# Attention output and forward keys of a gated linear attention block, turned by VectorE and trips through HBM in place of TensorE

## The chip, the cores and the metric

The kernel runs on one core of a Trainium2 chip. The time is the device time of one execution in microseconds; three runs of the kernel before are given. The profile is of one further execution, taken by the hardware profiler. Engines are PE (TensorE), DVE (VectorE), ACT (ScalarE), POOL (GpSimd) and SP (SyncE), which issues the DMAs.

## The reference, cut to what matters

One block over 1024 tokens of width 1024, all in float32. The input projection gives q, k (4 heads of 128), v, r (4 heads of 256), low-rank decays, a pooling input and two merge gates. The part around the change is the attention branch:

```python
def gla_chunked(q, k, v, log_a, include_diag):      # per head, in chunks
    b = jnp.cumsum(log_a...)                        # inside a chunk
    q_e = q * jnp.exp(b)
    k_e = k * jnp.exp(-b)
    k_d = k * jnp.exp(b_last - b)
    scores = jnp.where(mask, q_e @ k_e^T, 0.0)
    kv = k_d^T @ v                                  # sum over the chunk's tokens
    # state_{n+1} = exp(b_last) * state_n + kv_n
    return scores @ v + q_e @ state

o = gla(q, k, v, a_fwd, True) + flip(gla(flip(q), flip(k), flip(v), flip(a_bwd), False))
o = o * lax.rsqrt(jnp.mean(o * o, axis=-1, keepdims=True) + EPS)   # per head
o = o * gla_norm * silu(r)
y_a = o @ w_branch_gla
```

Two axes matter. The sum in kv runs over tokens, so keys are needed with tokens on the partitions, while q, k and their decays are computed with features on the partitions. The attention output o comes out with tokens on the partitions (the norm runs along its row), while `silu(r)` and the product with `w_branch_gla` want it with features there.

## The kernel before, in words

Tokens come in 8 tiles of 128 (two halves of 4), features in tiles of 128. Every float32 operand of a large product is split into a high and a low part; a product is three matmuls of 512 columns (hh x wh, hl x wh, hh x wl; `products` and `mm3`, line L273). Line L200 is the ACT cast that makes a high part, L201 the subtraction that makes the low part, on DVE or POOL (`split_to` for kt and p; the weights' wh and wl alike).

The order on each engine is written by hand. The main code runs the projections (q and k, v, then r, then the gates). After each three matmuls it calls `pump`, which advances the queues of side work: `side` (generators such as `attention(h)`; a `yield x` lets x units of main work pass before the next step), `aside`, `pending` and `put_off`. All engines execute in that order; SP too issues its DMAs in it, and each waits there for what it needs. `later` puts a store on a list, `flush` issues the list. Working tiles of 4 KB a row come from a pool of 39 (`slot`).

`attention(h)` runs for heads 0 to 3 in turn beside the projections; their backward loops begin at about 96, 160, 225 and 286 us. Its steps: the decays (la, z; with the scan of L851), the decayed q and k (qe, ke; d=0 is forward, d=1 backward), `transposed_keys` (four PE transposes into the PSUM tile kp, split into kt), then the backward loop n = 7 to 1. `advance` there takes kv on PE, st on DVE (L911, L913), and on ACT the state for this chunk sb (L917) and for the next step so (L921). Then `scores` (sc, its masking and its split p), and the forward loop n = 0 to 7: op on PE (p with v, then sb, then sf), another `advance`, the copy o (L999) on DVE, its squares (L1000) on ACT. `rms_scale` (DVE and a power on POOL) gives ors. The scalings by it (`normalize`, L1019) run in the next head, after its Exp, with stores to `o_out` by `flush`; in the last head they run at once, and o stays in SBUF.

The r projection (about 287 to 383 us) runs by feature tile j and half. For j below 3 the result is copied (`r`, L1236) and put by; from j = 3 each step does one of those and its own in `gated`: Silu on ACT, four PE transposes of o into the PSUM tile tp (L1188), one DVE instruction (L1195) that multiplies tp, the norm's weight and Silu(r). `load_o` reads heads 0 to 2 back as ol ahead of j = 2, 3, 4. Beside this stage run the gate projection's weights and sums (fraw, fs, L1093), and results of gates go through ga (L1474). Results of `gated` are stored to `ob_out`.

## Time and profile before

| | us |
|---|---|
| runs, median (lowest to highest) | 1374.98 (1374.72 to 1375.22) |
| span of the profiled execution | 1373.4 |
| PE busy | 1361.4 (99%) |
| DVE busy | 836.8 (61%) |
| POOL busy | 752.1 (55%) |
| ACT busy | 647.3 (47%) |

The profiled execution's own time is its span, 1373.4; the runs' median stands 1.6 above it. A row of the timeline reads: start, duration, engine, line, operation, output <- inputs, shape, count, and in brackets the idle time before it with the instruction that ended it. A row of a group reads: line, engine, operation, count | total, mean ns of one | idle time before, releaser. A row on a tile gives ns minimum/median/maximum and the first and last start. A window's row gives busy times of PE, PE's weight loads, DVE, ACT and POOL, then the granted clock, the DMA share and GB/s. Durations on one engine overlap a little, since an instruction starts before the one ahead has quite ended.

### The profile page before, as it was taken

What the parts mean: (1) busy time and instruction counts of PE and PEld (TensorE: products, weight loads), DVE (VectorE), ACT (ScalarE), POOL (GpSimd) and SP (SyncE); (2) the same over time, 40 slices, a digit from 0 to 9 for tenths busy, and PEclk for the clock granted to TensorE, in tenths of its full rate; (3) what the DMA queues carried; (4) which work ended last, traced back from release to release, by engine and by line L of the source; (5) the groups of instructions that cost most, each with busy time, mean ns of one, the idle gap of its engine ahead of it and who ended that gap; (6) DMA issues with size and microseconds to landing.
All of it is one profiled execution on the core that took longest, in us unless ns stands there. A gap on an engine that the chain in (4) does not pass through costs nothing. (4 is left out here: it accounts for less than half of the span.)

```text
span 1373.4 us, 17879 instructions
## 1 busy us (share of the span) xinstructions
PE 1361.4 (99%) x6310; PEld 1132.9 (82%) x6310; DVE 836.8 (61%) x1034; ACT 647.3 (47%) x1177; POOL 752.1 (55%) x557
## 2 busy tenths in 40 slices
PE   9999999999999999999999999999999999999998
PEld 7888888888888888888888888888888888888886
DVE  6974556554735777678883955655566556343375
ACT  7365666755534445554346533333333334444253
POOL 3323723222597547667764376666676667455454
PEclk9999999999999999999999999999999999999999
DMA  6321523314778569995416355555544447985451
GB/s 227 113 87 52 181 90 92 95 60 123 245 236 278 186 198 308 373 386 216 150 71 241 112 174 176 176 176 177 176 145 137 146 136 266 384 301 187 169 215 77
DMA packets 167834, 251.97 MB, mean 183 GB/s; under 512 B 11160, under 2 KB 94144, under 8 KB 167744
## 3 DMA queue, kind: packets, MB, share of 16 engines
q1 hardware_dynamic: 167600, 250.57, 53.8%
q8 instruction: 49, 0.80, 0.2%
q14 instruction: 41, 0.34, 0.1%
q10 hardware_dynamic: 144, 0.26, 0.0%
HBM read 168.74 MB, written 82.05 MB: 183 GB/s over the span
## 5 line engine op out<-in xcount | busy, mean ns | idle before, releaser
L201 POOL TENSOR_TENSOR wl<-fs,wh 128x512 fp32r<-128x512 f32 x124 | 173.1, 1400 | 163.5 <-ACT wh L200 104.0
L273 PE MATMUL ps<-gh,wh 128*128 128x512 f32 x616 | 240.5, 390 | 0.0
L273 PE MATMUL ps<-gl,wh 128*128 128x512 f32 x616 | 239.8, 389 | 0.3 <-DVE gl L1691 0.3
L273 PE MATMUL ps<-gh,wl 128*128 128x512 f32 x616 | 239.7, 389 | 0.0
L201 POOL TENSOR_TENSOR wl<-fraw,wh 128x512 fp32r<-128x512 f32 x93 | 134.0, 1442 | 75.0 <-ACT wh L200 72.4
L201 POOL TENSOR_TENSOR ol<-gor,oh 128x1024 fp32r<-128x1024 f32 (+1 forms) x42 | 101.3, 2417 | 86.0 <-ACT oh L200 71.7
L273 PE MATMUL ps<-hh,wh 128*128 128x512 f32 x356 | 145.1, 408 | 0.7 <-ACT ga L1474 0.7
L273 PE MATMUL ps<-hh,wl 128*128 128x512 f32 x356 | 139.0, 390 | 0.0
L273 PE MATMUL ps<-hl,wh 128*128 128x512 f32 x356 | 138.8, 390 | 0.0
L273 PEld LDWEIGHTS ps<-gl,wh 128*128 128x128 f32 x616 | 115.7, 188 | 24.5 <-DVE gl L1691 0.7
L273 PEld LDWEIGHTS ps<-gh,wh 128*128 128x128 f32 x616 | 115.7, 188 | 24.1 <-ACT hb L1710 0.2
L273 PEld LDWEIGHTS ps<-gh,wl 128*128 128x128 f32 x616 | 115.7, 188 | 23.9
L273 PE MATMUL ps<-oh,oh 128*128 128x512 f32 x308 | 119.8, 389 | 0.0
L273 PE MATMUL ps<-ol,oh 128*128 128x512 f32 x308 | 119.8, 389 | 0.0
L273 PE MATMUL ps<-oh,ol 128*128 128x512 f32 x308 | 119.8, 389 | 0.0
L201 POOL TENSOR_TENSOR wl<-wraw,wh 128x512 fp32r<-128x512 f32 x56 | 92.3, 1679 | 44.7 <-ACT wh L200 44.6
L201 POOL TENSOR_TENSOR wl<-raw,wh 128x512 fp32r<-128x512 f32 x34 | 47.4, 1404 | 108.3 <-ACT wh L200 71.9
L201 DVE TENSOR_TENSOR ol<-wor,oh 128x1024 fp32r<-128x1024 f32 (+1 forms) x42 | 62.8, 1506 | 68.1 <-ACT oh L200 55.5
L200 ACT CAST wh<-fs 128x512 fp32r<-128x512 f32 x124 | 76.1, 615 | 29.5 <-DVE fs L1093 28.3
L273 PEld LDWEIGHTS ps<-hh,wl 128*128 128x128 f32 x356 | 66.8, 188 | 14.4
L273 PEld LDWEIGHTS ps<-hh,wh 128*128 128x128 f32 x356 | 67.0, 188 | 13.1 <-ACT ga L1474 1.1
L273 PEld LDWEIGHTS ps<-hl,wh 128*128 128x128 f32 x356 | 67.0, 188 | 12.0
(281 smaller groups left out, 3073.4 us busy)
## 6 DMA issues: line engine op xcount, KB each, us to landing
fraw<-in_w_ffn_in_dram SPq DMA_DIRECT2D x44, 512.0 KB, 6.1
gor<-g_out SPq DMA_DIRECT2D x35, 512.0 KB, 6.1
fraw<-in_w_in_dram SPq DMA_DIRECT2D x22, 512.0 KB, 6.5
g_out<-s SPq DMA_DIRECT2D x44, 256.0 KB, 2.3
wor<-t_out SPq DMA_DIRECT2D x20, 512.0 KB, 3.7
raw<-in_w_in_dram SPq DMA_DIRECT2D x36, 256.0 KB, 5.1
g_out<-g SPq DMA_DIRECT2D x33, 256.0 KB, 2.6
x<-in_x_dram SPq DMA_DIRECT2D x16, 512.0 KB, 5.6
```

The costliest lines, as they stand in the source:

```text
L200: nc.scalar.copy(hi, src)
L201: eng.tensor_tensor(lo, src, as_f32(hi), op=ALU.subtract)
L273: nc.tensor.matmul(ps, a[i], b[j], start=first and n == 0, stop=last and n == 2, skip_group_check=onto)
```

## The change

Two kinds of transposes leave PE. A transpose of a 128x512 tile is instead made of two steps: DVE turns each 32x32 block in place (STREAM_TRANSPOSE), and four stores, one for each group of 32 partitions, write the blocks to their places in HBM in runs of 512 bytes; a load brings the tile back with the other axis on the partitions, its columns in blocks of 32.

- Forward keys (d=0): `turn_keys` after the backward keys of half 0 and at n = 6 of the backward loop, `put_keys` (4 stores of 64 KB) at n = 7 and 4, `get_keys` (256 KB) at n = 5 and 1, `split_keys` at n = 1 and in the forward loop at n = 2. The backward keys keep `transposed_keys`.
- Output: `turn` scales two tiles and turns them; half 0 in the forward loop (n = 5, 6), half 1 in the next head where `normalize` stood, in two steps. Each half is stored by 4 DMAs of 128 KB (two stores of 512 KB per head before). The last head's output goes the same way now: its stores are kept in `last_o` and issued at j = 4 of the r projection, and `load_o(3)` follows at j = 5. The rms scale is taken in two halves.
- `gated` has no PE transposes; four DVE instructions of 128x4x32 read the loaded tile and Silu(r), both in SBUF.

```diff
+        def turn_keys(half, d):
+            both = slot(s="kq")
+            nc.vector.transpose(
+                both[:, 0, :].rearrange("p (j c b) -> p c j b", j=4, b=SQ),
+                ke[half][:, d, :].rearrange("p (c j a) -> p c j a", j=4, a=SQ),
+            )
+            turned_k[half, d] = both
+        def put_keys(half, d):
+            to = k_out[h, half, d].rearrange("(j a) (i m) -> i a j m", a=SQ, i=4)
+            for i in range(4):
+                src = turned_k[half, d][i * SQ : (i + 1) * SQ, 0, :]
+                nc.sync.dma_start(to[i], src.rearrange("p (j m) -> p j m", j=4))
+        def get_keys(half, d):
+            nc.sync.dma_start(turned_k[half, d][:, 1, :], k_out[h, half, d])
+        def split_keys(half, d):
+            kt = slot(F32R, s="kt")
...
+            split_to(hi, lo, back)
+            kts[half, d] = kt
...
         kts[0, 1] = transposed_keys(0, 1)
+        turn_keys(0, 0)
...
             if n == 7:
                 apply_decay(1, 0)
+                put_keys(0, 0)
+            elif n == 6:
+                turn_keys(1, 0)
+            elif n == 5:
+                get_keys(0, 0)
+            elif n == 4:
+                put_keys(1, 0)
+            elif n == 1:
+                split_keys(0, 0)
+                get_keys(1, 0)
             yield 1.2
             if n == 3:
-                kts[0, 0] = transposed_keys(0, 0)
                 yield 0.5
...
+        def turn(half, part):
...
+            for i in range(2 * part, 2 * part + 2):
+                t = o[half][:, i, :]
+                nc.vector.tensor_scalar(t, t, scales[half][:, i : i + 1], None, op0=ALU.mult)
+            nc.vector.transpose(
+                turned[half][:, :, :].rearrange("p k (n b) -> p n k b", b=SQ)[:, two],
+                o[half][:, two, :].rearrange("p n (k a) -> p n k a", a=SQ),
+            )
+            if part:
+                to = o_out[h][half].rearrange("(k a) (i m) -> i a k m", a=SQ, i=4)
+                for i in range(4):
+                    (last_o if h == HEADS - 1 else deferred).append((to[i], turned[half][i * SQ : (i + 1) * SQ, :, :]))
...
             if n == 0:
                 yield 0.38
-                kts[1, 0] = transposed_keys(1, 0)
...
+            if n == 2:
+                split_keys(1, 0)
             if n == 3:
                 p = q_next
+                scales[0] = rms_scale(ms[:, :4], 4, "ors")
+            if n in (5, 6):
+                turn(0, n - 5)
...
-        tp = bank(ps_g, "tp")
-        for i in range(4):
-            nc.tensor.transpose(
-                tp[:, i * P : (i + 1) * P],
-                o_heads[j // 2][half][:, i, (j % 2) * P : (j % 2 + 1) * P], ident[:, :],
-            )
...
+        for i in range(4):
+            nc.vector.scalar_tensor_tensor(
+                every(tiles[half][:, j % 2, :], i), turned[:, i], g_gla[:, j : j + 1], every(sr[:, :], i),
+                op0=ALU.mult, op1=ALU.mult,
+            )
...
             if half == 0:
                 flush()
+                if j == 4:
+                    deferred.extend(last_o)
+                    flush()
+                elif j == 5:
+                    load_o(HEADS - 1)
```

What moves on the engines, at the three places that matter most. First SP in head 3, from its weights to the loads of earlier heads' output (raw is a piece of weights, ol an output read back, k_out and kq the turned keys in HBM and in SBUF). Before:

```order
L208 DMA raw_2832<-in_w_in_dram 128x4x128
L208 DMA raw_2834<-in_w_in_dram 128x4x128
L1033 DMA ol_2961<-o_out_565 128x1024
L1033 DMA ol_2962<-o_out_565 128x1024
L208 DMA raw_2965<-in_w_in_dram 128x4x128
L208 DMA raw_2967<-in_w_in_dram 128x4x128
L1033 DMA ol_3151<-o_out_566 128x1024
L1033 DMA ol_3152<-o_out_566 128x1024
L208 DMA raw_3155<-in_w_in_dram 128x4x128
L208 DMA raw_3157<-in_w_in_dram 128x4x128
```

and now:

```order
L209 DMA raw_2898<-in_w_in_dram 128x4x128
L209 DMA raw_2900<-in_w_in_dram 128x4x128
L926 DMA k_out_571<-kq_2999 32x4x128 x4
L1091 DMA ol_3033<-o_out_573 128x2x512
L1091 DMA ol_3034<-o_out_573 128x2x512
L209 DMA raw_3037<-in_w_in_dram 128x4x128
L209 DMA raw_3039<-in_w_in_dram 128x4x128
L929 DMA kq_2999<-k_out_571 128x512
L926 DMA k_out_572<-kq_3055 32x4x128 x4
L929 DMA kq_3055<-k_out_572 128x512
L1091 DMA ol_3218<-o_out_574 128x2x512
L1091 DMA ol_3219<-o_out_574 128x2x512
```

Ahead of the first ol and of the raw behind it now stand the four stores of half 0's turned keys.

Second ACT in head 3, the last four steps of the backward loop (wh and raw: weights of the r projection; kt: split keys; p: split scores). Before:

```order
L200 CAST wh_3010<-raw_2965 128x512
L917 ACTIVATE sb_2946<-st_3018,fac_2859 128x256
L921 ACTIVATE so_3021<-st_3018,fac_2859 128x256
L200 CAST wh_3029<-raw_2967 128x512
L200 CAST kt_3038<-kp_3033 128x512
L917 ACTIVATE sb_2946<-st_3045,fac_2859 128x256
L921 ACTIVATE so_3048<-st_3045,fac_2859 128x256
L917 ACTIVATE sb_2946<-st_3057,fac_2859 128x256
L1236 COPY r_2969<-ps_2970 128x512
L200 CAST p_3078<-sc_3069 128x512
```

and now:

```order
L201 CAST wh_3089<-raw_3037 128x512
L951 ACTIVATE sb_3014<-st_3097,fac_2925 128x256
L955 ACTIVATE so_3100<-st_3097,fac_2925 128x256
L201 CAST wh_3108<-raw_3039 128x512
L951 ACTIVATE sb_3014<-st_3116,fac_2925 128x256
L955 ACTIVATE so_3119<-st_3116,fac_2925 128x256
L951 ACTIVATE sb_3014<-st_3128,fac_2925 128x256
L201 CAST kt_3131<-kq_2999 128x512
L1300 COPY r_3041<-ps_3042 128x512
L201 CAST p_3153<-sc_3144 128x512
```

The cast of kt has left the middle of the loop and stands behind its last sb, and reads the tile loaded from HBM (kq) instead of kp.

Third DVE in head 2, the end of the forward loop (from the st of n = 3 on; o is the copy of the output). Before:

```order
L913 SCALAR_TENSOR_TENSOR st_2598<-kv_2594,fac_2273,so_2580 128x256
L999 COPY o_2493<-op_2588 128x256
L913 SCALAR_TENSOR_TENSOR st_2623<-kv_2619,fac_2318,so_2601 128x256
L999 COPY o_2494<-op_2613 128x256
L913 SCALAR_TENSOR_TENSOR st_2644<-kv_2640,fac_2318,so_2626 128x256
L999 COPY o_2494<-op_2634 128x256
L913 SCALAR_TENSOR_TENSOR st_2665<-kv_2661,fac_2318,so_2647 128x256
L999 COPY o_2494<-op_2655 128x256
L999 COPY o_2494<-op_2676 128x256
```

and now:

```order
L947 SCALAR_TENSOR_TENSOR st_2677<-kv_2673,fac_2367,so_2652 128x256
L1061 COPY o_2550<-op_2667 128x256
L947 SCALAR_TENSOR_TENSOR st_2698<-kv_2694,fac_2367,so_2680 128x256
L1061 COPY o_2550<-op_2688 128x256
L1037 TENSOR_SCALAR o_2549<-o_2549,ors_2657 128x256 x2
L1038 STREAM_TRANSPOSE ot_2706<-o_2549 128x2x8x32
L947 SCALAR_TENSOR_TENSOR st_2723<-kv_2719,fac_2367,so_2701 128x256
L1061 COPY o_2550<-op_2713 128x256
L1037 TENSOR_SCALAR o_2549<-o_2549,ors_2657 128x256 x2
L1038 STREAM_TRANSPOSE ot_2706<-o_2549 128x2x8x32
L1061 COPY o_2550<-op_2737 128x256
```

Two scalings and a block transpose stand ahead of the last st, and two more and another ahead of the last copy; before, all eight scalings came after the loop.

More of the change, by code (lines that the diff above doesn't have):

```diff
@@ L29 @@
 SUB = 64
+SQ = 32
 GROUPS = 4
@@ L731, in finish_beside @@
             aside.pop(0)
-    o_heads, unscaled = {}, []
+    k_out = {
+        (h, half, d): dram.tile([P, HALF], F32, name=f"k_out{h}{half}{d}")
+        for h in range(HEADS) for half in range(2) for d in range(1)
+    }
+    o_heads, unscaled, last_o = {}, [], []
     HOLD, SCORES = 5.0, 6
@@ L902, in transposed_keys @@
             return kt
+        turned_k = {}
+        def turn_keys(half, d):
[14 more added lines that the diff above has]
+            kt = slot(F32R, s="kt")
+            hi, lo = (kt[:, i, :].rearrange("p (c i b) -> p c i b", c=4, b=SQ) for i in range(2))
+            back = turned_k[half, d][:, 1, :].rearrange("p (i c b) -> p c i b", i=4, b=SQ)
+            split_to(hi, lo, back)
+            kts[half, d] = kt
         def advance(old, n, d, kt, dst, ends=False):
@@ L984, in attention @@
         old = sf = None
+        scales, turned = {}, {}
+        def turn(half, part):
+            if part == 0:
+                turned[half] = slot(shape=(DV // SQ, 4 * SQ), s="ot")
+            two = slice(2 * part, 2 * part + 2)
+            for i in range(2 * part, 2 * part + 2):
[9 more added lines that the diff above has]
+                    (last_o if h == HEADS - 1 else deferred).append((to[i], turned[half][i * SQ : (i + 1) * SQ, :, :]))
         for n in range(NT):
@@ L1194, in gated, with every @@
         tiles, there = oT[j // 2]
-        nc.vector.scalar_tensor_tensor(
-            tiles[half][:, j % 2, :], tp[:, :], g_gla[:, j : j + 1], sr[:, :], op0=ALU.mult, op1=ALU.mult
-        )
+        def every(t, i):
+            return t.rearrange("p (n i b) -> p i n b", n=4, b=SQ)[:, i]
+        turned = o_heads[j // 2][half][:, j % 2, :].rearrange("p (i n b) -> p i n b", i=4, b=SQ)
+        for i in range(4):
[3 more added lines that the diff above has]
+            )
         there.append((j, half))
```

30 lines of the change are left out of this document (13 added, 17 removed).

## Prediction

> **What bounds the kernel now.** I read first the busy table of the page, then the waits of TensorE (PE), then the groups by line, last the timelines around every place that the change touches. Times are microseconds.
>
> ```profile
> PE 1361.4 (99%) x6310; PEld 1132.9 (82%) x6310; DVE 836.8 (61%) x1034; ACT 647.3 (47%) x1177; POOL 752.1 (55%) x557
> ```
>
> ```profile
> PE ps L273 <- ACT ga L1474: 0.7, 1, 0.7
> PE ps L273 <- POOL wl L201: 0.6, 2, 0.4
> PE op L273 <- DVE p L201: 0.4, 2, 0.2
> ...
> PE op L273 <- ACT p L200: 0.3, 1, 0.3
> ```
>
> PE is busy for 99% of the span, and the waits shown (line, releaser: total, times, longest) are under 1. So an instruction taken from PE is worth its issue time, as long as nothing becomes late that PE now finds ready. The three rows naming wl and p are places where the side work has no slack already.
>
> **Part 1: transposes taken off PE.** Out go 8 of the 16 groups of four at L899 (forward keys, two per head) and all 64 at L1188.
>
> ```profile
> L899 PE MATMUL kp<-ident,ke 128*128 128x128 f32 x64 | 9.6, 272 | 0.0
> ```
>
> ```profile
> L1188 PE MATMUL tp<-ident,ol x48: 272/273/273, 319.9 to 352.5; 128*128 128x128 f32 x48
> L1188 PE MATMUL tp<-ident,o x16: 270/272/273, 360.8 to 382.6; 128*128 128x128 f32 x16
> ```
>
> Durations overlap in PE's pipeline, so I price a pair of groups by starts:
>
> ```profile
> 319.68 0.40 PE L273 MATMUL ps<-hh,wl 128*128 128x512 f32 x1
> 319.91 1.04 PE L1188 MATMUL tp<-ident,ol 128*128 128x128 f32 x8
> ...
> 321.02 0.39 PE L273 MATMUL ps<-hl,wh 128*128 128x512 f32 x1
> 321.25 0.40 PE L273 MATMUL ps<-hh,wl 128*128 128x512 f32 x1
> ```
>
> From 319.68 to 321.25 go three steps of 0.23 (321.25 less 321.02), 0.69, and eight transposes: 1.57 - 0.69 = 0.88, so a group of four is 0.44; L899's cost the same (272 and 273 ns). L1188's 48 run as 6 pairs (6 x 0.88 = 5.3), its other 16 as 4 groups (1.8), the keys as 8 (3.5): **-10.6**. Of this the group at the backward loop of head 1 is lost again: value weights (wl) are ready just when PE asks (the 0.4 in the waits), and an earlier PE waits longer: **+0.4**.
>
> **Part 2: VectorE's block transposes (DVE).** The trace has none; for 128x512 I bound one by 0 and by the dearest 128x512 row quoted below (1.26), and take 0.69, the lo subtraction of kt, as the nearest in size and operands. Of the 16 for the output, eight stand in the forward loops (n = 5 and 6), behind two scalings each:
>
> ```profile
> 254.98 0.48 DVE L913 SCALAR_TENSOR_TENSOR st<-kv,fac,so 128x256 f32<-128x256 f32 x1 [1.45 <-ACT op L1000]
> ```
>
> ```profile
> L1019 DVE TENSOR_SCALAR o<-o,ors 128x256 f32<-128x256 f32 x32 | 9.8, 380 | 1.8 <-POOL ors L305 1.8
> ```
>
> The hole of 1.45 ahead of st holds 2 x 0.38 + 0.69 = 1.45, just; the other eight sit between heads, where the same scalings stood. I add **+0.3** for the last st of four heads. Only the first turn of a head stands ahead of an st. At the dear end, 1.26, that st is 0.6 late; over four, 2.3 if PE took all of it; at the cheap end nothing is lost. The rms scale in two parts is two more small instructions on POOL per head, long before their use: nothing. Eight stores of the output at 0.59 in place of two put some 4 more on SP between heads; the value weights behind them are loaded ahead, and no PE wait names a DMA: nothing, though with a store's landing on top one weight of head 1 can come a few tenths late. "VectorE: DVE Perf Modes" of the Trainium skill, "The three transpose paths", gives 311 ns for a 128x128 bf16 transpose on VectorE; four of that make 1.24 (an estimate), with which that st is 0.55 late and the 0.3 would be up to 2.2. No row here shows one.
>
> **Part 3: forward keys through HBM.** Per half: one DVE transpose, four stores of 64 KB in 512-byte pieces, one load of 256 KB, ACT's cast and DVE's subtraction from SBUF in place of PSUM (0.6 and 0.7 as before). Nearest rows: uraw (16x4x128, 512-byte pieces) for the stores' issue and landing; for the load the page's u_out row, whose 256 KB lie in whole rows, and as its late end raw.
>
> ```profile
> L373 SPq DMA_DIRECT2D uraw<-in_w_decay_up_bwd_dram x4: 592/592/593, 24.9 to 26.8; - x4
> ...
> DMA to landing us min/median/max: 2.6/3.3/4.1
> ```
>
> ```profile
> wh<-u_out SPq DMA_DIRECT2D x14, 256.0 KB, 3.6
> ```
>
> ```profile
> L208 SPq DMA_DIRECT2D raw<-in_w_in_dram x28: 367/453/1477, 20.5 to 312.0; - x28
> ...
> DMA to landing us min/median/max: 3.0/5.1/5.8
> ```
>
> The turn stands behind the lo of the backward keys (kt), which ends 0.6 after its row starts; then 0.7 for the turn, four issues (4 x 0.59 = 2.4), landing 3.3, load 3.6. The split comes 0.5 behind the last sb of the loop. Heads 0, 1 and 2:
>
> ```profile
> 95.45 0.68 DVE L201 TENSOR_TENSOR kt<-kp,kt 128x512 fp32r<-128x512 f32 x1
> ...
> 159.50 0.68 DVE L201 TENSOR_TENSOR kt<-kp,kt 128x512 fp32r<-128x512 f32 x1
> ...
> 222.64 0.68 DVE L201 TENSOR_TENSOR kt<-kp,kt 128x512 fp32r<-128x512 f32 x1
> ```
>
> ```profile
> 106.46 0.51 ACT L917 ACTIVATE sb<-st,fac 128x256 f32<-128x256 f32 x1 [0.56 <-DVE st L913]
> ...
> 172.42 0.51 ACT L917 ACTIVATE sb<-st,fac 128x256 f32<-128x256 f32 x1 [0.55 <-DVE st L913]
> ...
> 235.67 0.51 ACT L917 ACTIVATE sb<-st,fac 128x256 f32<-128x256 f32 x1
> ```
>
> ```profile
> 161.44 10.87 SPq L694 DMA_DIRECT2D s_out<-wsum  x4
> ```
>
> Loaded at 95.45 + 10.6 = 106.05, at 171.1 (170.1, and 1.0 for the s_out in front of it on SP) and at 233.2. The split is due at about 105.9, 170.5 and 235 (last sb plus 0.5 for itself and 0.5 for turn_keys, less the 1.6 that the loop wins, next paragraph; 2.9 in head 1 with a wait there, and 1.1 in head 2, where turn_keys delays nothing): the two fall together in heads 0 and 1, head 2 has 1.8. The second half has many microseconds: nothing.
>
> And the cast and subtraction leave the middle of the backward loop:
>
> ```profile
> 291.54 0.48 DVE L913 SCALAR_TENSOR_TENSOR st<-kv,fac,so 128x256 f32<-128x256 f32 x1 [0.98 <-ACT so L921]
> 294.00 0.69 DVE L201 TENSOR_TENSOR kt<-kp,kt 128x512 fp32r<-128x512 f32 x1 [1.97 <-ACT kt L200]
> 294.60 0.47 DVE L913 SCALAR_TENSOR_TENSOR st<-kv,fac,so 128x256 f32<-128x256 f32 x1
> ```
>
> A step of this chain is 1.46 (the first row's 0.98 and 0.48); here it took 3.06, so 1.6 are won, 0.5 given back by turn_keys ahead of the first st. The waits for p (0.3 and 0.4, heads 1 and 2) go: **-0.7**.
>
> **Part 4: head 3, where SP falls behind.** SP issues in order. Now it is ahead of its time here: weights (raw) go out at 270.5, with the outputs of earlier heads (ol) around them, and ACT, also in order, casts them at 291 to 293.
>
> ```profile
> 270.50 1.63 SPq L208 DMA_DIRECT2D raw<-in_w_in_dram  x2
> ```
>
> ```profile
> 291.41 0.61 ACT L200 CAST wh<-raw 128x512 fp32r<-128x512 f32 x1
> ...
> 297.46 0.59 ACT L200 CAST p<-sc 128x512 fp32r<-128x512 f32 x1
> ```
>
> ```profile
> 284.79 0.68 DVE L201 TENSOR_TENSOR kt<-kp,kt 128x512 fp32r<-128x512 f32 x1
> ...
> 298.08 0.69 DVE L201 TENSOR_TENSOR p<-sc,p 128x512 fp32r<-128x512 f32 x1 [0.94 <-ACT p L200]
> ```
>
> ```profile
> 300.12 0.28 PE L273 MATMUL op<-vh,p 128*128 128x256 f32 x1
> ```
>
> After the change four k_out stores stand ahead of both ol and both raw, and wait for a transpose behind the kt of 284.79: 285.4 + 0.7 = 286.1. Stores to 288.5, ol to 289.3, raw at 289.3 and 289.8; landing by the raw row at 292.3 (3.0) to 295.6 (5.8). With 1 MB of ol just ahead I take 295.4, near the late end. ACT waits at its 291.41 cast, and sb, so, the split, the copy of r and p behind it. From the cast to p's end now is 298.77 - 291.41 = 7.4; less about 1.1 (kt gone, split added) 6.3. So p ends at 301.7; PE wants it at 300.12 - 0.44 = 299.7: **+2.0**. Ends: 0, since landing at 292.3 gives 298.6, and 2.2 by the 5.8; 3 if ol lands late too.
>
> **Part 5: the r stage and after.** SP moves 2 MB more around 340 to 370 (last head's stores put off and read back), and gated's one DVE instruction becomes four of 128x4x32, each with two SBUF operands.
>
> ```profile
> 350.00:360.00 10.00, 10.00 (x50) 8.35 (x49) 9.97 (x9) 5.86 (x10) 5.65 (x5) 1.00 0.99 317
> ```
>
> ```profile
> L1093 DVE TENSOR_TENSOR fs<-fraw 128x512 f32<-128x512 f32 x31 | 39.1, 1261 | 10.1 <-POOL wsum L713 7.1 <-POOL wl L201 2.5 <-DMA fraw<-in_w_in_dram 0.6
> ...
> L1093 DVE TENSOR_TENSOR fs<-fs,fraw 128x512 f32<-128x512 f32 x31 | 24.6, 793 | 0.1
> ```
>
> In that window DVE (third pair, 9.97 of 10) and DMA (0.99, 317 GB/s) are full, and just behind it stands PE's wait of 0.7 on ACT ga. 1 MB ahead of the queue there is 1.05/317 = 3.3: ends 0 and 3.3. Most consumers there have over 2.5 of slack; only a store's landing that ga waits for and one hs load have none. I take **+1.0**. The same operation on DVE took 793 and 1261 ns by its neighbours. The Trainium skill, "SBUF — State Buffer", section "Who interferes with whom", says that a VectorE instruction with two SBUF inputs contends with a GpSimd instruction that reads SBUF; the two rows agree. By that rule gated's new form, which had one operand in PSUM, would be stretched by as much as 1.6 (1261 over 793); the case stands in C.
>
> **Sum.** -10.6 + 0.4 + 0.3 - 0.7 + 2.0 + 1.0 = -7.6. The span of 1373.4 becomes 1365.8; the runs' median stands 1.6 above the span, so **1367.4**.
>
> **Rivals.** (A) As summed; its own range is 1365 to 1370.
> (B) Full gain: raw lands in time (3.0) and the r stage hides its DMAs, so 2.0 + 1.0 drop out: 1364.4. For it: the landing minimum of raw. Against: 1 MB ahead of it in one queue.
> (C) The r stage takes the whole 3.3, and gated's longer DVE work makes 1 late in the full window, at most the 2.5 of slack: 1367.4 + 2.3 + 1 = 1370.7, up to 1372.2.
> (D) The other side: the trips are slow in heads 0 to 2. ACT is in order, so a split that waits for its load holds p, and PE behind it. Head 0's p ends here:
>
> ```profile
> 107.68 0.69 DVE L201 TENSOR_TENSOR p<-sc,p 128x512 fp32r<-128x512 f32 x1 [0.65 <-ACT p L200]
> ```
>
> ```profile
> 109.90 0.28 PE L273 MATMUL op<-vh,p 128*128 128x256 f32 x1
> ```
>
> That leaves 1.5, or 1.1 with PE 0.44 earlier, and 1.1 are won. If store and load each take x longer than assumed, PE loses 2x - 2 in head 0, 2x - 1 in head 1, 2x - 2.8 in head 2. At x = 1.8 that is 1.6 + 2.6 + 0.8 = 5.0, and the gain is lost within measurement; from x = 2.7 (3.4 + 4.4 + 2.6 = 10.4) the kernel is slower; x = 3.5 gives 15.2, 1382.6. For it: the raw row's 5.8 is 2.2 over my load, the stores' 4.1 is 0.8 over my store. Against: both are the latest ends of their rows, and the mean of the two is 1.5.
>
> **How the numbers follow.** About 0.2%, 2.75, is what a measurement can tell: faster is below 1372.2, slower above 1377.7. A 0.46, B 0.18, C 0.14 (0.02 of it at or above 1372.2), D 0.22 (0.03 below 1372.2, 0.09 between, 0.10 slower). Faster 0.46 + 0.18 + 0.12 + 0.03 = 0.79, same 0.11, slower 0.10. The range goes from 1363 (below B, transposes a little dearer than priced) to 1376, inside D; outside are 0.04 and 0.13.
>
> **What would show it.** Right: 96 fewer PE instructions; no PE wait on p in heads 1 and 2, one of 1 to 3 near 300 behind an ACT cast of raw; st steps of 1.46 throughout the backward loops. Wrong: ACT kt waiting on a load of k_out in head 0 or 1 (D), new PE waits on ga, wl or trh after 350 (C), a DVE transpose over 0.9, or no wait near 300 (B). The forecast fails most easily on the length of a trip, since two follow each other and no row shows a 32-partition store of 64 KB.

## The result, and the profile after

| | before | after |
|---|---|---|
| runs, median (lowest to highest) | 1374.85 (1374.69 to 1375.22) | 1386.72 (1386.16 to 1387.22) |
| span of the profiled execution | 1373.4 | 1385.4 |
| PE busy | 1361.4 | 1357.3 |

The ratio is 1.0085, with an interval of 1.0073 to 1.0097. The change makes the kernel slower by 11.9 us where 7.6 less were forecast; the time lies outside the range and on the other side.

The busy table of the page after, in the form of the one before:

```profile
PE 1357.3 (98%) x6214; PEld 1127.2 (81%) x6214; DVE 865.0 (62%) x1110; ACT 647.1 (47%) x1177; POOL 756.0 (55%) x561
```

PE issues 96 instructions fewer, as forecast, but is busy only 4.1 less, and 12.0 more of span means 16.1 more idle time. The waits of PE after (line, releaser: total, times, longest) say where it is:

```profile
PE ps L274 <- ACT ga L1538: 10.5, 2, 9.8
PE op L274 <- ACT p L201: 3.3, 3, 1.1
PE sc L963 <- DVE st L947: 2.8, 1, 2.8
...
PE ps L274 <- POOL wl L202: 1.3, 2, 1.1
PE op L274 <- DVE p L202: 0.7, 3, 0.2
PE op L1060 <- ACT sf L951: 0.6, 2, 0.4
```

There are three new places: one wait of 9.8 in the r stage (ga, before 0.7), one wait before p in each of heads 1, 2 and 3, and one of 2.8 in the backward loop of head 1 (st). The steps that the change added were not dear themselves. The groups on DVE (count | total, mean ns) and the DMA rows (KB each, median us to landing) after:

```profile
L1253 DVE SCALAR_TENSOR_TENSOR o<-ol,cols,sr 128x128 f32<-128x128 f32 x64 | 27.4, 497 | 16.9 <-ACT sr L1243 14.4 <-POOL wl L202 2.4
...
L1038 DVE STREAM_TRANSPOSE ot<-o 128x512 f32<-128x512 f32 x16 | 11.4, 712 | 0.6
...
L916 DVE STREAM_TRANSPOSE kq<-ke 128x512 f32<-128x512 f32 x8 | 5.6, 702 | 6.2 <-POOL qe L890 6.2
```

```profile
o_out<-ot SPq DMA_DIRECT2D x32, 128.0 KB, 2.5
ol<-o_out SPq DMA_DIRECT2D x8, 512.0 KB, 4.7
...
k_out<-kq SPq DMA_DIRECT2D x32, 64.0 KB, 1.8
kq<-k_out SPq DMA_DIRECT2D x8, 256.0 KB, 2.7
```

A block transpose takes 0.70 to 0.71 (0.69 assumed), a store of keys lands in 1.8 (3.3 assumed) and their load in 2.7 (3.6 assumed). The 6.2 of idle time before L916 is a single wait, and the first sign of the cause in head 1.

### Three places in the trace of after

**Head 1, the turn of half 1 (cause S, a tile of the full pool).** Timeline of after, DVE, ACT and POOL:

```profile
162.58 0.48 DVE L947 SCALAR_TENSOR_TENSOR st<-kv,fac,so 128x256 f32<-128x256 f32 x1 [1.85 <-ACT so L955]
...
168.02 1.26 POOL L890 TENSOR_TENSOR qe<-qe,q 128x512 f32<-128x512 f32 x1
...
169.32 0.71 DVE L916 STREAM_TRANSPOSE kq<-ke 128x512 f32<-128x512 f32 x1 [6.25 <-POOL qe L890]
169.95 0.44 DVE L947 SCALAR_TENSOR_TENSOR st<-kv,fac,so 128x256 f32<-128x256 f32 x1
170.43 0.51 ACT L951 ACTIVATE sb<-st,fac 128x256 f32<-128x256 f32 x1 [6.42 <-DVE st L947]
```

The turn reads ke, which is ready, and does not read qe; yet POOL's qe releases it. Its new tile kq is the place in the working pool that q had, and the last reader of q is that qe, which POOL reaches only at 168.02. DVE is in order, so st behind the turn waits 6.25 too, then sb, and PE by 2.84 at the scores (sc; their PSUM bank comes from the pool of kv, which st reads). That the place is q's is inferred: q is what this qe reads for the last time. The old kernel met the same wait here, for kt, three steps later in the loop, where POOL was nearly done:

```profile
169.22 0.59 ACT L200 CAST kt<-kp 128x512 fp32r<-128x512 f32 x1 [1.69 <-POOL qe L882]
```

**Heads 1 to 3, the split of the keys (cause P).** Timeline of after, the end of the backward loop in head 1:

```profile
175.76 0.48 DVE L947 SCALAR_TENSOR_TENSOR st<-kv,fac,so 128x256 f32<-128x256 f32 x1 [0.98 <-ACT so L955]
...
176.69 0.60 ACT L201 CAST kt<-kq 128x512 fp32r<-128x512 f32 x1
177.33 0.69 DVE L202 TENSOR_TENSOR kt<-kq,kt 128x512 fp32r<-128x512 f32 x1 [1.09 <-DMA s_out<-wsum]
177.94 0.69 DVE L968 COPY_PREDICATED sc<-keep,sc 128x512 f32<-128x512 uint8 x1
178.66 0.59 ACT L201 CAST p<-sc 128x512 fp32r<-128x512 f32 x1 [1.36 <-DVE sc L968]
...
179.29 0.39 PE L274 MATMUL op<-vh,p 128*128 128x256 f32 x1 [1.14 <-ACT p L201]
```

The load is in time (no wait of kt for k_out; the subtraction's row names a store, but the cast that it follows ends at 177.29). But the split stands ahead of the mask of the scores on DVE, and takes its turn through ACT and then DVE; the mask comes behind it, p behind the mask. The last st of the loop starts at 175.76, so p's cast is 2.90 behind it. Before, in the same head, it was 1.12:

```profile
171.90 0.48 DVE L913 SCALAR_TENSOR_TENSOR st<-kv,fac,so 128x256 f32<-128x256 f32 x1 [0.98 <-ACT so L921]
173.02 0.59 ACT L200 CAST p<-sc 128x512 fp32r<-128x512 f32 x1
```

**The r stage (causes H, L and C, as below).** SP, ACT and DVE, timeline of after; hs are pieces read for the third operand (trh), whose cast stands ahead of gated's Silu and of the copy ga on ACT:

```profile
337.51 13.07 SPq L674 DMA_DIRECT2D hs<-f_out  x2
350.64 0.90 SPq L564 DMA_DIRECT2D ob_out<-o  x2
351.83 1.06 SPq L674 DMA_DIRECT2D hs<-f_out  x1
352.95 2.15 SPq L1091 DMA_DIRECT2D ol<-o_out  x2
...
362.11 1.04 ACT L708 CAST trh<-hs 128x1024 fp32r<-128x1024 f32 x1 [6.18 <-DMA hs<-f_out]
363.72 4.24 DVE L1253 SCALAR_TENSOR_TENSOR o<-ol,cols,sr 128x128 f32<-128x128 f32 x8 [3.63 <-ACT sr L1243]
368.59 0.62 ACT L201 CAST wh<-fs 128x512 fp32r<-128x512 f32 x1 [3.40 <-DVE fs L1151]
369.12 0.58 ACT L1538 COPY ga<-ps 128x512 f32<-128x512 f32 x1
```

PE waits from 359.96 to 369.75 for that ga. The chain before it: the hs load is late (6.18), eight pieces of gated take 4.24, and wh waits behind them for fs (3.40). The first row holds the oldest lateness: 13.07 for two issues, which spanned 9.89 before. SP's own waits from 330 to 375 name it:

```profile
SPq L674 <- PE ps L274: 12.8, 2, 12.5
```

and the same two issues before, the second of which then waited 9.1 for trl on DVE:

```profile
333.27 9.89 SPq L673 DMA_DIRECT2D hs<-f_out  x2
```

The fifth hs load, the second of these two, now takes the place of a hidden-state tile that PE reads until about 350. Everything that SP issues later stands behind it, ol and the next hs loads included.

### The clock

PE's wait is not the whole price. Windows of after (third from the end is PE's granted clock), around the ends of the two longest waits:

```profile
170.00:171.00 1.00, 0.55 (x2) 0.55 (x3) 0.40 (x2) 0.57 (x2) 0.92 (x2) 0.63 0.08 20
171.00:172.00 1.00, 1.00 (x7) 1.00 (x6) 0.48 (x1) 0.45 (x2) 1.00 (x1) 0.50 0.57 137
...
370.00:375.00 5.00, 5.00 (x12) 3.88 (x13) 2.22 (x4) 3.16 (x5) 4.91 (x3) 0.50 0.69 278
375.00:378.00 3.00, 2.96 (x13) 2.09 (x11) 3.00 (x7) 1.11 (x3) 1.56 (x1) 0.99 0.00 0
```

In head 1 (behind the 2.84, and a wait of 1.11 for wl that ended 3.6 earlier) the clock is about half for 3.3 us of work, and behind the r stage's wait for 5.3: some 1.5 and 2.6 lost, 4.1 in all (half of each busy time, with the parts of a window in proportion).

So, of the span's +12.0: -10.6 as priced, +16.1 of waits, +4.1 of clock, and 2.4 that these do not explain; a part of that is found below.

### The profile page after: what moved, and what is told of

The parts are those of the page before. It is cut to its first block, busy times and chain, and to the rows that moved or that the text cites. A ratio compares the mean times of both kernels' runs of the same rounds, so it can differ in the third digit from the quotient of the medians.

```text
span 1385.4 us, 17846 instructions
## 1 busy us (share of the span) xinstructions
PE 1357.3 (98%) x6214; PEld 1127.2 (81%) x6214; DVE 865.0 (62%) x1110; ACT 647.1 (47%) x1177; POOL 756.0 (55%) x561
## 5 line engine op out<-in xcount | busy, mean ns | idle before, releaser
L202 POOL TENSOR_TENSOR wl<-raw,wh 128x512 fp32r<-128x512 f32 x34 | 50.8, 1505 | 87.8 <-ACT wh L201 80.9
L274 PE MATMUL ps<-trh,wh 128*128 128x512 f32 x176 | 69.6, 396 | 9.8 <-ACT ga L1538 9.8
```

What stands on the lines that cost most here:

```text
L202: eng.tensor_tensor(lo, src, as_f32(hi), op=ALU.subtract)
L274: nc.tensor.matmul(ps, a[i], b[j], start=first and n == 0, stop=last and n == 2, skip_group_check=onto)
```

## The experiments

In all of them the kernel before ran on the same chip at about 1375.0. "ga" is PE's longest wait for ga. Short names: P and S are the causes above; H is the place that the hs load waits for; L the last head's trip in the r stage (its stores, its tiles, and its read-back among the hs loads); C the second SBUF operand of gated on DVE beside POOL (none of these letters is a rival of the prediction). First, single parts of the change undone or moved.

**e1: the split moved behind the scores.**

```diff
             elif n == 1:
-                split_keys(0, 0)
                 get_keys(1, 0)
...
         p = scores(0)
+        split_keys(0, 0)
```

> The changed kernel with one move: the split of half 0's turned keys stands behind scores(0) instead of in front of it. Theory P (order of the split): in heads 1, 2 and 3 the cast and the subtraction of kt stand between the last st and the mask of the scores, so p is 1.5 later and PE waits 1.1 + 0.2 for it; moved, those three waits on p go and the time falls by 3 to 4.5, to 1382 to 1384. Theory D of the prediction (the trips are late): the split waits for its load, so the wait only moves behind p to the first kv, and the time stays at 1386 to 1387.

Measured: 1382.48 (1381.83 to 1383.72), ratio 1.0056 (1.0039 to 1.0073): 4.2 won, and no wait for p in any head. In head 1, ACT after the edit:

```profile
175.90 0.51 ACT L951 ACTIVATE sb<-st,fac 128x256 f32<-128x256 f32 x1 [0.55 <-DVE st L947]
176.50 0.59 ACT L201 CAST p<-sc 128x512 fp32r<-128x512 f32 x1
176.99 0.62 ACT L201 CAST kt<-kq 128x512 fp32r<-128x512 f32 x1
```

p's cast follows sb at once. P is shown: 4.0 of waits (3.3 and 0.7), 4.2 of time. Head 3's wait for p went too, though raw stays late there (ACT waits 2.33 for it), so the late raw alone costs PE nothing (nor in e10, where ACT waits 2.42 for it).

**e2: the turn of half 1 three steps later.**

```diff
-            elif n == 6:
-                turn_keys(1, 0)
...
-            elif n == 4:
-                put_keys(1, 0)
+            elif n == 3:
+                turn_keys(1, 0)
+            elif n == 2:
+                put_keys(1, 0)
```

> The changed kernel with the turn of half 1's keys at n = 3 and its stores at n = 2 of the backward loop, instead of n = 6 and 4. Theory S (a working tile): in head 1 this turn gets the tile that held q, which POOL reads until 169.3 behind weights; DVE executes in order, so st and everything behind it stood for 6.3. At n = 3 POOL is done, PE's waits of 2.8 (sc on st) and some of the 1.1 (op on p) in head 1 go, and the low clock behind them: the time falls by 3 to 6, to 1381 to 1384. Rival: POOL is late for another reason and st would have waited anyway, or half 1's load now comes too late for the forward loop's n = 4: no gain, 1386 to 1388.

Measured: 1384.52, ratio 1.0073 (1.0058 to 1.0088): 2.2 won, between the two theories. The wait for st is gone, but p in head 1 now costs 3.21. ACT in head 1:

```profile
169.30 0.51 ACT L951 ACTIVATE sb<-st,fac 128x256 f32<-128x256 f32 x1 [3.85 <-POOL qe L890]
```

Another tile, an sb, now waits for the same qe, so q's place has gone to it. It is the place, not the turn, that holds the loop: S's mechanism is shown, and moving the turn only passed the place on.

**e3: the last head's output stays in SBUF and is turned by PE.**

```diff
         (last head) turn(half, part)
+        scalings alone, as before; o_heads[h] = o, no last_o, no load_o(HEADS - 1)
         (gated, j // 2 == HEADS - 1)
+        tp = bank(ps_g, "tp") and four nc.tensor.transpose, one product of 128x512
```

> The changed kernel, but the last head's output is scaled in place, stays in SBUF and is transposed by TensorE in gated (four groups of four, 1.8 of PE), as before the change; its 2 MB of stores and loads and its four extra working tiles are gone. Theory L (the last head's trip): its tiles and its load stand ahead of the hs and fraw loads on SP, these come late, and ga with them; the wait of 9.8 on ga and the low clock behind it go, and the time falls by 8 to 12 to 1375 to 1379. Theory C (DVE): gated's instructions with two SBUF operands are what makes ga late; 48 of the 64 stay, so at most a third of the loss goes: 1382 to 1386.

Measured: 1384.04, ratio 1.0067 (1.0052 to 1.0082); ga 4.9 in place of 9.8, 2.7 won with 16 transposes put back (1.8 as priced). The last head's trip is a part of the r stage's wait, but half stays without it. Neither theory had that. The edit takes away stores, tiles and read-back together, so which of them counts stays open.

**e4: only the output's part of the change, forward keys on PE.**

```diff
-        turn_keys(0, 0)
...
             if n == 3:
+                kts[0, 0] = transposed_keys(0, 0)
...
             if n == 0:
+                kts[1, 0] = transposed_keys(1, 0)
```

> Only the output's part of the change: all keys turned by TensorE as before (3.5 of PE back), output through HBM as in the changed kernel. If the losses in heads 1 to 3 come from the keys' part alone (theories P and S), the time falls by 3.5 to 7.5 net, to 1379 to 1383, and the wait on ga of about 10 stays. If the output's stores and turns make heads 1 to 3 late, it stays at 1386 or above.

Measured: 1377.84 (1376.66 to 1378.63), ratio 1.002 (1.0011 to 1.0029). The waits for p and st are as before; ga 6.9, 2.9 less than in after, which neither theory had: a part of that wait comes from the keys' trips too. So the keys' trips cost 8.9 of the 11.9, and the output's part alone is 2.8 slower than before; its added waits lie in the r stage but for 0.5 at wl.

**e5: e4 with Silu(r) in PSUM.**

```diff
-        sr = t2(s="sr")
+        sr = bank(ps_g, "sr")
```

> All keys on TensorE and the output through HBM (the run before it of that kind: 1377.8, with PE's wait of 6.9 on ga), and Silu(r) written to a PSUM bank, so that gated's four DVE instructions have one operand in SBUF instead of two. Theory C (contention with POOL): single ones of these took 1.3 to 1.4 instead of 0.34 while POOL ran, and eight of them 5 where two took 1.4 before; now all take about 0.35, fs and ga come 2 to 3 earlier, POOL's wl of 4.6 at 326 to 331 is back to 1.3, and the time falls by 2.5 to 4, to 1374 to 1375.5. Theory L (last head's trip alone): the wait on ga stays above 6, 1377 to 1378.

Measured: 1375.28, ratio 1.0001 (0.9992 to 1.0011), ga 4.9. The 64 pieces of gated take 344 ns in place of 497:

```profile
L1242 DVE SCALAR_TENSOR_TENSOR o<-ol,cols,sr 128x128 f32<-128x128 f32 x64 | 17.4, 344 | 15.4 <-ACT sr L1232 14.2 <-POOL wl L202 1.2
```

C is worth 2.6 of time here. Both sides pay: where 20 such pieces run on DVE at 332, two weights on POOL take 5.84 after and took 2.55 before.

```profile
334.04 5.84 POOL L202 TENSOR_TENSOR wl<-raw,wh 128x512 fp32r<-128x512 f32 x2 [4.42 <-DMA o_out<-ot]
```

```profile
327.71 2.55 POOL L201 TENSOR_TENSOR wl<-raw,wh 128x512 fp32r<-128x512 f32 x2 [5.39 <-ACT wh L200]
```

In e5 the same pair takes 2.55 again.

What is left of the wait is nearly all PE's lead. Copies to ga in the old kernel and in e5:

```profile
357.16 0.58 ACT L1474 COPY ga<-ps 128x512 f32<-128x512 f32 x1
```

```profile
357.50 0.58 ACT L1527 COPY ga<-ps 128x512 f32<-128x512 f32 x1
```

The copy is only 0.3 later than before. But PE, which came to it at 358.10 then, just behind the copy, now comes at 353.19, and waits 4.94 until 358.13.

**e6: e4 with the last head on PE (the edit of e3).**

```diff
 e4, and
+            o_heads[h] = o      (last head; no turn, no last_o, no load_o(HEADS - 1))
+            tp = bank(ps_g, "tp") and four nc.tensor.transpose in gated, where j // 2 == HEADS - 1
```

> All keys on TensorE, output of heads 0 to 2 through HBM, the last head's output kept in SBUF and transposed by TensorE (1.8 of PE back). Theory L: the hs load that trh waited 3.4 for at 353 lands in time, the wait on ga falls from 6.9 by 3 to 4 and with it the stretch of low clock; net of the 1.8 the time falls by 1 to 3, to 1375 to 1377. Theory C alone: the wait stays at 6 to 7, and the time rises by 1 to 2, to 1379 to 1380.

Measured: 1377.14, ratio 1.0016 (1.0006 to 1.0025), ga 4.9. Without L the wait is 2.0 shorter, and the transposes give 1.8 back: 0.7 of time, no gain clear of the intervals.

**e7: e5 with the last head's read-back behind all hs loads, into o's own tiles.**

```diff
-                elif j == 5:
-                    load_o(HEADS - 1)
...
                 for _ in range(2):
                     gunits[1].load()
+                load_o(HEADS - 1)
...
+            o_heads[HEADS - 1] = o's two tiles, seen as [2, 512]
```

> All keys on TensorE, output of all heads through HBM, Silu(r) in PSUM, and the last head's output read back behind the hs and fraw loads of the r stage instead of between them, into the tiles that it came from. If C and L together are the loss of the r stage, PE's wait on ga falls to 0 to 1.5 with no low clock, and the output's part gives what it takes off PE: 1375.0 less 7.1, plus about 0.5 for the weights in head 1: 1368 to 1370. If something else holds ga (DMA volume as such), 1372 to 1376.

Measured: 1375.86, ratio 1.0005 (0.9996 to 1.0014), ga 5.6, 0.7 more than e5. A miss: the hs loads, freed from ol, wait for another place (SP's L674 for ACT's sr, 7.4, and for PE, 8.6). So the read-back's position alone is not L.

**e8: e7 with the forward keys of half 1 alone through HBM.**

```diff
-        turn_keys(0, 0)   (half 0 by transposed_keys again)
...
+            elif n == 2:
+                turn_keys(1, 0)
+                put_keys(1, 0)
...
         p = scores(0)
+        get_keys(1, 0)
```

> As the run above it, and the forward keys of half 1 alone through HBM (turned and stored at n = 2 of the backward loop, loaded behind the scores), half 0 on TensorE as before. One working tile more is alive, but only behind the n = 3 step. Theory S (the tile that is full in head 1 is the one taken between n = 7 and n = 3): no new wait in the heads, the four groups give 4 x 0.44 = 1.8: 1366 to 1368.5. If any trip of keys costs a wait in heads 1 to 3, it is no faster than the run above, 1368 to 1373.

Measured: 1377.73, ratio 1.002 (1.0011 to 1.0029). Four groups of transposes less than e7 and 1.9 slower: ga 6.3, and new waits for sf behind the loop (1.8 in three, the longest 1.2). A miss too: sf's waits (in heads 0 and 1) and 0.7 more on ga cost more than the fewer transposes give. Why sf is late there was not traced.

**e9: before, with the 64 transposes of the output left out and sr in PSUM.** gated reads o as it lies, without any turn.

```diff
-        tp = bank(ps_g, "tp") and four nc.tensor.transpose
+        same = o_heads[j // 2][half][:, :, (j % 2) * P : (j % 2 + 1) * P]
-            tiles[half][:, j % 2, :], tp[:, :], ...
+            tiles[half][:, j % 2, :], same, ...
```

> The kernel before the change with the 64 output transposes on TensorE left out and nothing put in their place: gated's one DVE instruction reads o as it lies (that part of the result is not the reference's), Silu(r) in PSUM so that it has one SBUF operand as before. No added DMA, tile or DVE instruction. Theory R (the r stage is bound beside PE): hs loads, fs sums and the ga copy follow each other without regard to PE's lead, so the 7.1 taken off PE turn into a wait on ga of 4 to 5 and a stretch of low clock behind it, and the time is 1373 to 1375.5. Theory V (what the trip adds, DMAs and DVE work, is what makes ga late): no wait on ga above 1, and the time falls to 1367.5 to 1369.

Measured: 1369.61 (1369.46 to 1369.68), ratio 0.996 (0.9946 to 0.9974). PE is busy 1354.6, 6.8 less, where 7.1 was priced. ga 1.8: of the wait, 1.8 comes from PE's lead alone, with no trip at all. That lies between the two theories.

**e10: before, with the keys of heads 0, 2 and 3 through HBM, split late, head 1 and the output on PE.**

```diff
+        trip = h != 1      (ahead of each turn, put, get; transposed_keys where not)
...
         p = scores(0)
+        if trip:
+            split_keys(0, 0)
```

> The kernel before, with the forward keys of heads 0, 2 and 3 through HBM (split behind the scores), head 1's and the whole output on TensorE as before. Six groups of four leave PE: 2.6. Theories P and S (order of the split; the full tile pool of head 1): no wait of more than 0.3 is added in the heads, and the time falls by 1.5 to 2.6, to 1372.4 to 1373.5; by theory R some of it may come back as a wait on ga, 1373.5 to 1375. Theory D (trips late as such): new waits on p or kt in heads 0 or 2, 1375 to 1378.

Measured: 1373.82 (1372.75 to 1374.36), ratio 0.9989 (0.9979 to 0.9998): 1.3 won, ga 0.7, no new wait in the heads. Without P and S the trips are hidden. But PE is busy only 1.4 less (1360.0) for 24 transposes, where 2.6 was priced.

**e11: after, with the edits of e1, e5 and e7 together.**

```diff
-                split_keys(0, 0)               (to behind scores(0), e1)
-        sr = t2(s="sr")
+        sr = bank(ps_g, "sr")
-                    load_o(HEADS - 1)          (to behind both gunits[1].load(), into o's tiles, e7)
```

> The whole change with every mend at once: split behind the scores, Silu(r) in PSUM, the last head's output read back behind the r stage's loads into its own tiles. 10.6 off PE stands. Left: the wait in head 1 (2.8 with 0.7 on wl and low clock) and the r stage. By theories P and C: 1378.5 to 1380.5 (from 1382.5 less 2 to 4). If the r stage's wait disappears with all three: 1371 to 1374. If it is PE's lead that turns into that wait (theory R), the wait on ga stays at 7 or more.

Measured: 1381.41, ratio 1.0048 (1.0033 to 1.0063), ga 8.7, st 2.8. Only 1.1 better than e1, where PSUM alone won 2.6 between e4 and e5. So a cause common to all of them was still missing in the r stage. The wait above 7 is what theory R has; the time lies above the range of P and C.

**e12: e6 with sr in PSUM for the first three heads.**

```diff
-        sr = t2(s="sr")
+        sr = bank(ps_g, "sr") if j // 2 < HEADS - 1 else t2(s="sr")
```

> All keys on TensorE; output of heads 0 to 2 through HBM with Silu(r) in PSUM, the last head's output in SBUF and on TensorE with Silu(r) in SBUF. 48 transposes (5.3) off PE. Theories C and L add: the wait on ga, 6.9 with neither mend and 4.9 with either, falls to 2 to 3.5, no low clock, time 1373 to 1374.5. Theory R sets a floor: PE still has 5.3 of lead, so a wait of 4 to 5 stays and the time is 1375 to 1376.

Measured: 1377.99, ratio 1.0021 (1.0012 to 1.003), ga 4.9. C and L do not add: either brings ga from 6.9 to 4.9, both leave it there, and the time is above every forecast. The floor of 4.9 is H, as e13 and e14 show.

**e13: e5 with the hs loads from the fifth on in tiles of earlier ones.**

```diff
-                wholes.append(slot(s="hs"))
+                wholes.append(slot(s="hs") if len(wholes) < 4 else wholes[-3])
```

> All keys on TensorE, all output through HBM, Silu(r) in PSUM (that run: 1375.3, wait on ga 4.9), and the fifth to eighth hs load of the r stage go into the tiles of the second to fourth instead of fresh ones, so that they wait for trl on DVE and not for TensorE's last read of the hidden state. Theory H (the tile): the fifth load goes out at about 340 instead of 343.5, trh no longer waits 3.4 on a load, the wait on ga falls to 1.5 to 3 and the low clock goes: 1370.5 to 1373. Rival (DMA volume: 1 MB of ol and 1 MB of stores more): the loads still land late, 4.5 or more on ga, 1374.5 to 1376.

Measured: 1371.88 (1371.12 to 1373.35), ratio 0.9979 (0.9969 to 0.9988): 3.1 faster than before, the best of the versions that do the whole computation. SP's waits from 330 to 375 in e13, to set beside after's:

```profile
SPq L674 <- DVE trl L699: 17.0, 4, 9.5
```

No hs load waits for PE. The fifth goes out at 340.42, in e5 at 343.47 (before at 342.85). The copy to ga that PE waits for starts at 354.45 in place of 357.50, and ga's wait is 2.0 in place of 4.9, near the 1.8 of e9. H is shown; the edit also takes four tiles less from the pool, and no run separates that. The low clock did not go: a second wait of 1.97 is followed by it (last section).

**e14: e12 with the line of e13.**

```diff
 e12, and
-                wholes.append(slot(s="hs"))
+                wholes.append(slot(s="hs") if len(wholes) < 4 else wholes[-3])
```

> The same reuse of tiles with the last head's output kept in SBUF and on TensorE (without it: 1378.0, wait on ga 4.9). No extra load or store in the r stage, so theory H gives the 1.8 that remained when transposes were simply left out, less the 1.8 of PE work kept: wait on ga 1 to 2, 1371 to 1373. Rival (lead of PE and DVE's four instructions for one): 3.5 or more on ga, 1375 to 1377.

Measured: 1373.18, ratio 0.9988 (0.9978 to 0.9997), ga 2.7, longer than theory H had it. With H gone the last head's trip is, if anything, the better choice: without it the kernel is 1.3 slower than e13, near the price of its transposes, though the two intervals overlap.

**e15: e13 with the keys of heads 0, 2 and 3 through HBM, split late.**

```diff
 e13, and
+        trip = h != 1      (ahead of each turn, put, get; transposed_keys where not)
+        if trip:
+            split_keys(0, 0)               (behind scores(0))
```

> All causes found removed together: forward keys of heads 0, 2, 3 through HBM with the split behind the scores, head 1's on TensorE, output through HBM, Silu(r) in PSUM, hs loads reusing their tiles. 9.7 is off PE. If each cause stands alone: waits of 2 to 3.5 on ga, under 1 in the heads, 1368 to 1372. If the keys' tiles and the output's tiles together fill the pool elsewhere: new waits in the heads of 2 or more, 1373 to 1377.

Measured: 1372.79 (1370.99 to 1373.87), ratio 0.9983 (0.9974 to 0.9992), ga 3.9, no wait above 0.4 in the heads. No better than e13, and between the two forecasts: the longer wait takes back what the keys give, with the clock at 0.50 behind it.

**e16: after with the line of e13 alone.**

```diff
 after, and
-                wholes.append(slot(s="hs"))
+                wholes.append(slot(s="hs") if len(wholes) < 4 else wholes[-3])
```

> The changed kernel (1386.7) with the reuse of hs tiles alone. Theory H: the wait on ga falls from 9.8 by 2.5 to 5 and some of the low clock with it, while the waits in the heads stay: 1380 to 1384. Rival (contention and the last head's load carry the r stage): 9 to 10 stays, 1385 to 1388.

Measured: 1383.36, ratio 1.0061 (1.0044 to 1.0077), ga 5.9 in place of 9.8. H is worth 3.4 in the change as made.

**e17: e13 with sr in SBUF.**

```diff
-        sr = bank(ps_g, "sr")
+        sr = t2(s="sr")
```

> e13 with Silu(r) in SBUF again: gated's four DVE instructions have two SBUF operands, hs loads reuse their tiles, all keys on TensorE. Theory C (contention with POOL counts by itself): single ones of 1.3 to 1.4 again, the first wait on ga 3.5 to 5.5 and a stretch of low clock, 1373.5 to 1376 against 1371.9. Theory H alone (only the loads mattered): 1371.5 to 1373.

Measured: 1375.41, ratio 1.0002 (0.9993 to 1.0012), ga 5.2. Against e13, C alone is 3.5 of time and 3.2 of wait; POOL's pair of weights takes 5.85 here and 2.56 in e13.

**e18: e13 with the read-back of e7.**

```diff
 e13, and
-                elif j == 5:
-                    load_o(HEADS - 1)          (to behind both gunits[1].load(), into o's tiles)
```

> e13 with the last head's output read back behind the r stage's hs and fraw loads, into the tiles it came from. If its 1 MB holds up the load that ga waited 2.0 for at 362.8, that wait falls to 0.7 and the clock stays full behind it: 1369 to 1371. If the DMA engines are simply full there (0.97 to 1.07 from 345 to 360 but for one stretch), it moves to another wait: 1371.5 to 1373.5.

Measured: 1377.0, ratio 1.0014 (1.0004 to 1.0023), ga 6.6: 5.1 worse than e13. A miss, outside both ranges. SP's waits from 330 to 375:

```profile
SPq L674 <- ACT sr L1234: 8.4, 1, 8.4
```

An hs load again takes a place whose last reader is late, this time Silu's input r. Which change of the pool's order hands it that place was not traced.

## Why the prediction failed, point by point

- **Part 1, -10.6: right for the output, too high for the keys.** The 64 transposes and their price of 7.1 stand against 6.8 of busy time in e9. For 24 transposes of keys e10 shows 1.4 against 2.6; in proportion the 32 are worth 1.9, not 3.5. With the output's 0.3 that is 1.9 of the 2.4 unexplained above; the other 0.5 stays open, and so does why the keys' transposes are worth so little. The +0.4 at wl was 0.7 (1.11 in place of 0.44), but 0.5 of it comes with the output's part (0.90 in e4), not from the keys' group.
- **Part 2, +0.3: right in kind.** The turns take 0.70 to 0.71, and PE waits 0.6 for sf in the forward loops of heads 0 and 1. In head 0 the two scalings ahead of the last st took 1.63 where 0.76 was assumed. With all keys on PE (e4) the same turns cost no wait for sf, so the output's part alone gave 0 here. The estimate of 1.24 from the Trainium skill, "VectorE: DVE Perf Modes", section "The three transpose paths", does not hold for this shape; the measurement decides.
- **Part 3, the time of the trips: right; rival D wrong.** They are shorter than assumed, and no split waits for its load in heads 0 to 2.
- **Part 3, "the cast and subtraction leave the middle of the backward loop ... The waits for p (0.3 and 0.4, heads 1 and 2) go: -0.7": the first step that failed.** The 1.6 won in the loop is there, but where the two land was not followed: ahead of the mask, on the path to p, for 2.90 - 1.12 = 1.8 in head 1. In place of -0.7 came +3.3 (4.0 of waits for p where 0.7 were): 4.2 of time in e1. The order shows kt ahead of p on ACT. The working looked at whether kt's data is there in time, and only Part 4 counts the added cast (0.5 on ACT); that kt's subtraction then stands ahead of the mask on DVE is counted nowhere.
- **The sum had no term for the pool's places.** "one DVE transpose" was costed by its duration and its operands. Its output's place has a last reader too: S, 2.8 of wait and some 1.5 of clock. The same kind of wait is H, worth 3.4 in e16.
- **Part 4, +2.0: right on ACT, wrong on PE.** raw is late as forecast, though by less (ACT waits 2.49 at 300.64 in after and 2.33 in e1, where 295.4 - 291.41 = 4.0 was assumed), but with p's path clear PE does not wait: 0.
- **Part 5, +1.0 with ends 0 and 3.3: the term most mis-sized.** The wait grew by 9.1, and the clock took 2.6 more. The ends came from bytes ahead of the queue; what held the queue was a place that PE still read (H), and what held the chain behind was C and, in a part that stays open, L. Rival C of the prediction had the stage and the contention, but with 1 to 2.5 for the latter (3.5 in e17) and 3.3 for the bytes. The cover of the +1.0, "Most consumers there have over 2.5 of slack", was measured before PE was made 7 faster in front of it. e9 shows 1.8 of wait from that lead alone, and e5 4.9 with a copy to ga that is only 0.3 later than before.
- **The clock was not in the sum.** Waits were counted at their length; two of them cost 4.1 more.

For the contention the rows are POOL's 2.55 against 5.84 beside DVE's 20 pieces, and 497 against 344 ns on DVE with one operand in PSUM. The Trainium skill, "SBUF — State Buffer", section "Who interferes with whom", says that a VectorE instruction with two SBUF inputs contends with a GpSimd instruction that reads SBUF, and one with at most one SBUF input, outside the two-port modes, does not; the traces agree (a piece takes up to 1439 ns in after and at most 348 in e5).

What was not tried: after with the place of S taken away while head 1's keys keep their trip. So S's own share of time is known only from its wait and its clock, not from a run.

## What to carry to other kernels

An added working tile in a full pool costs what its place costs: ask which instruction reads the old tile last, and on which engine, before counting the new instruction's duration. Work moved out of a loop lands somewhere: put it behind the next step that the critical engine waits for, not ahead of it. When the bounding engine is made faster in one stage, subtract the gain from the slack of every chain that meets it there; e13 kept 3.1 of about 7 after two repairs (C and H), and e15's further lead was waited away.

## What was not expected of the hardware

The granted clock falls behind waits of PE that are short. e14's wait of 2.70 ends at 355.47, and its windows behind it are:

```profile
355.40:356.00 0.60, 0.53 (x2) 0.48 (x3) 0.60 (x2) 0.60 (x3) 0.60 (x1) 1.00 1.07 310
356.00:357.00 1.00, 1.00 (x4) 0.77 (x3) 0.65 (x3) 1.00 (x2) 1.00 (x1) 0.61 1.14 330
357.00:358.00 1.00, 1.00 (x3) 0.73 (x3) 1.00 (x1) 1.00 (x2) 1.00 (x2) 0.50 1.15 316
```

Here the clock drops some 0.7 after PE is at work again (0.61 over the second window). Waits of 1.8 (e9) and 2.01 (e13, first) left it at 1.00; e13's second, of 1.97 and ending at 362.79, was followed by three windows at 0.50:

```profile
355.10:357.00 1.90, 1.90 (x8) 1.60 (x9) 1.90 (x2) 1.39 (x2) 1.90 (x2) 1.00 0.94 300
...
364.00:365.00 1.00, 1.00 (x4) 0.81 (x3) 1.00 (x2) 0.00 (x0) 1.00 (x1) 0.50 0.34 135
```

Even one of 1.49 was (e3, in head 3, ending at 307.31, with 0.50 from 310 to 312), where the three for p in after (1.05 to 1.14) were not. So waits of 1.5 to 2 can go either way here, and each of the waits from 2.7 up (2.70, 2.84, 3.21, 3.89, 4.94, 9.79 among them) was followed by half clock, mostly for 3 to 5 us of work. The Trainium skill, "TensorE: Matmul & The Clock Gate", "Part 1: The HAM clock gate", has the half rate after at least one idle window of about 3.4 us, a window that runs free of the kernel; the runs agree on the half rate, and like waits with unlike outcomes fit a window of free phase, but they show the half rate after waits shorter than that window.
